# HGRN's first decays moved into ACT's, DVE's and POOL's queues ahead of its chunk loop, early tiles in DRAM, products queued at fixed places among the dense matmuls

## The chip, the cores and the metric

The kernel runs on one core of one Trainium2 chip. The metric is the device time of one execution in microseconds (us); before the change the median of three runs is 858.56 us (858.18 to 858.79). Engines: PE is TensorE (PEld its weight load), DVE VectorE, ACT ScalarE, POOL GpSimd, SP the queue that issues the weight loads. Each engine takes its instructions in the order that the build wrote, and stands when the first of them is not ready.

## The reference

One decoder layer over 512 tokens of width 1024, fp32. Two mixers run side by side on the same normed input, are merged by sigmoid gates, and a SwiGLU FFN follows. The change is in the mixers:

```
b = cumsum(log f)                       # HGRN2, 4 heads of 128, per chunk
decay[i,j] = exp(b_i - b_j), j <= i
attn = einsum(q_i, k_j, decay)
o = attn v + (q exp(b)) S
S = S exp(b_last) + (k exp(b_last - b))^T v
o_a = head_rms_norm(o) * silu(hg_g)

q, k = l2norm(silu(conv(q))), l2norm(silu(conv(k)))   # gated DeltaNet, 4 heads of 128
T = inverse(I + strict_lower(beta k k^T L))           # per chunk
v_new = u - w S;  o = qg S + (q k^T L) v_new;  S = S dl + kd^T v_new
o_b = head_rms_norm(o) * silu(dn_g)

merged = sigmoid(m_a) * (o_a Wa) + sigmoid(m_b) * (o_b Wb)
```

## The kernel before

Every dense product is made of three fp32r matmuls on a high and a low half of each operand (`mm3`). `dense_in` makes one feature tile (128 features by 512 tokens) at a time: `wload` loads 512 KB of weights (SP), casts the high half on ACT (whi, L108) and subtracts it on DVE (wlo, L109); 24 matmuls of 128x512 (two of L116 and one of L117 for each of eight rows of blocks) then fill one of three "mm" PSUM banks, and an evacuation (ACT, DVE or both) empties it. Three buffers each hold whi and wlo.

`mixers` writes the work down in program order, and a scheduler at build orders each engine's queue from it by its own estimate of when operands are ready; `high_priority` moves instructions forward, `issue_after` keeps one behind a named other one. So PE's queue is a fixed mixture: small products are set among dense matmuls. The stages around the change, with their place in the trace:

- 60 to 84 us: l2 norm of k (`l2`, `colsum`: square on ACT, split into halves by an ACT cast (L120) and a DVE subtraction, two matmuls with a matrix of ones (L376, L377) into a "dps" bank, Ln and Exp on ACT, multiplication on DVE) among the tiles of hg_f. `gates_late` (small exps of the DeltaNet gates, L337 to L347) reads gb, which comes by DMA. `dn_early` then builds k k^T and POOL's part begins: a copy through DRAM (L427, L429), 62 small substitution steps (`dn_sub`), and the copies of `dn_inv` through DRAM (L458 to L486), which end at 162 us.
- 84 to 177 us: dn_q, dn_v, dn_g, the l2 norm of q, `hg_prep` (HGRN's k and cumulative log decay b for four chunks on ACT and DVE, temporary "hct" tiles), hg_q's four tiles and two of hg_g (`qe`, `gge`), kept in six of the seven hct buffers; `dn_inv`'s products among the dense ones.
- 177 to 256 us: DeltaNet's `dn_prep` and four `dn_step`s in "dct" tiles (nine buffers), with the gate m_b0 among them, whose tiles go to DRAM (`gate_out`, early_b). POOL copies the early q and g out of the hct buffers into slots that come free (L792, L794): the slot of kT, which DeltaNet's last reads free, and that of qT.
- 256 to 370 us: HGRN. `hg_attn` makes one chunk's attention matrix: the diagonal and level 1 by two column sums, then for levels 64, 32, 16, 8, 4, 2 a tile E = exp(differences of b) (two subtractions on POOL, exp on ACT L660), multiplied on DVE by q in one half and by k in the other, and products of E with itself into one of two "hps" banks (L667 for 64 and 32, L673 for the rest), from which AT is patched (L669, L674). `hg_step` does output and state (L684, L693, L698, L704) and the head norm. The loop makes chunk c + 1's matrix beside chunk c's step. The dense work hg_g (two tiles), y_dn (`y_proj`) and m_b1 stands behind in program order, and the scheduler puts it where it believes PE free.

The rest (m_a, y_hg, merge, output projection, FFN, down projection) is not touched.

Of the kernel before, what the change touches and what calls it, by code (L numbers as in the profile page):

```python
# [43 lines left out]
class K:  # L44
# [324 lines left out]

    def colsum(self, sq, ct, ps, n=512, after=None):  # L370
# [4 lines left out]
        with self.tc.issue_after(after.ins) if after else nullcontext():  # L375
# [208 lines left out]
    def head_norm(self, c, o, gate, dst, ct, ps):  # L584
# [8 lines left out]
        sp = self.colsum(r, ct, ps)  # L593
# [36 lines left out]
    def hg_attn(self, c, out):  # L630
# [12 lines left out]
        E = self.hct((P, NH, 64))  # L643
# [8 lines left out]
        for lev in HG_LEVELS[:-1]:  # L652
            v = lambda x: x.rearrange("p h (n two t) -> p (h n) two t", two=2, t=lev)
            n = NH * P // (2 * lev)
            E = self.hct()
            Ev, bv, qv, kv = v(E), v(b), v(q), v(k)
            ref = bv[:, :, 0, lev - 1:lev].to_broadcast([P, n, lev])
            self.tt(Ev[:, :, 1, :], bv[:, :, 1, :], ref, ALU.subtract, nc.gpsimd)
            self.tt(Ev[:, :, 0, :], ref, bv[:, :, 0, :], ALU.subtract, nc.gpsimd)
            A.activation(E, E, AF.Exp)  # L660
            self.tt(Ev[:, :, 1, :], Ev[:, :, 1, :], qv[:, :, 1, :], ALU.mult)
            self.tt(Ev[:, :, 0, :], Ev[:, :, 0, :], kv[:, :, 0, :], ALU.mult)
            ps = self.hps()
# [8 lines left out]
            for h in range(NH):  # L672
                T.matmul(ps[:, h, :], E[:, h, :], E[:, h, :], start=True, stop=True)  # L673
# [3 lines left out]
    def hg_step(self, c, AT):  # L677
# [4 lines left out]
        o = self.hps()  # L682
        for h in range(NH):
# [41 lines left out]
    def mixers(self):  # L725
# [43 lines left out]
        for c in range(NC_):  # L769
            self.dn_prep(c)  # L770
# [530 lines left out]
```

## Time and profile before

| | |
|---|---|
| median of three runs | 858.56 us (858.18 to 858.79) |
| the profiled execution: time, span | 856.74 us, 855.0 us |
| mean granted clock of PE | 0.988 |
| busy: PE, DVE, ACT, POOL | 96%, 68%, 57%, 16% of the span |

The span runs from the first to the last instruction; the execution's own time is 1.7 us longer. A row of a timeline gives start, duration (the sum over xN instructions of a row that holds several), engine, line, operation, out<-in, shape, and in brackets how long the engine stood before and what released it. PE's busy time is modelled from starts, so two neighbours overlap in the rows; the distance of starts is what one costs. A clock of 1.00 is the higher of TensorE's two levels (2.4 GHz), 0.5 the lower (1.2).

### The profile page before, as it was taken

The numbers are of one execution on the slowest core, as the hardware profiler recorded it, in microseconds if no ns is written. First come the engines' busy times: TensorE is split into PE (matmuls) and PEld (weight loads), VectorE is DVE, ScalarE is ACT, GpSimd is POOL, SyncE is SP. The second block draws the span as 40 slices with busy tenths as digits, with TensorE's granted clock in tenths as the row PEclk, the third lists the DMA queues.
The fourth block names the chain that finished last, engine by engine and source line by source line (L and its number), as shares of the span: only waits on it lengthen the run. The fifth ranks groups of instructions, "written<-read, shape, count | busy, mean of one in ns | idle before, by whom it ended". The sixth has DMA issues, their size and how long they took to land.

```text
span 855.0 us, 12316 instructions
## 1 busy us (share of the span) xinstructions
PE 821.0 (96%) x4677; PEld 689.3 (81%) x4677; DVE 585.6 (68%) x903; ACT 485.4 (57%) x884; POOL 136.9 (16%) x187
## 2 busy tenths in 40 slices
PE   9998999999997999899999999999999998999995
PEld 8886887767876877788888898999999997876774
DVE  4794998625557788862664797787787787557545
ACT  6658798945376466585443365545455456445443
POOL 1420178300034245430010300000000000000000
PEclk9998999999999999999999999999999999999999
DMA  8425532712126112253211313322413404556552
GB/s 294 153 94 177 140 108 74 179 51 74 38 86 209 51 49 87 87 173 97 86 53 49 123 50 100 116 82 99 145 54 99 148 24 141 181 172 206 186 175 99
DMA packets 34907, 98.53 MB, mean 115 GB/s; under 512 B 4192, under 2 KB 4608, under 8 KB 34720
## 3 DMA queue, kind: packets, MB, share of 16 engines
q1 hardware_dynamic: 32112, 88.65, 31.5%
q0 software_dynamic: 2736, 9.09, 4.0%
q8 instruction: 37, 0.61, 0.3%
q14 instruction: 22, 0.18, 0.1%
HBM read 91.95 MB, written 5.78 MB: 114 GB/s over the span
## 4 chain that ended last, share of the span: by engine, by line
PE 66%; DVE 12%; DMA 11%; ACT 6%; issue 3%; POOL 0%; SPq 0%; DVEq 0%; ACTq 0%; POOLq 0%
PE mm L116 20%; PE mm L117 11%; DMA raw<-in_w_down_dram 8%; DVE wlo L109 3%; PE hps L116 3%; ACT whi L108 3%; DVE hct L146 3%; PE hps L1041 2%; PE hps L1040 2%; PE hps L1042 2%; PE hps L117 2%; DVE s L149 2%; PE hps L673 2%; DVE s L146 1%; PE mm L898 1%
## 5 line engine op out<-in xcount | busy, mean ns | idle before, releaser
L116 PE MATMUL mm<-s,whi 128*128 128x512 f32 (+1 forms) x992 | 310.5, 392 | 0.0
L109 DVE TENSOR_TENSOR wlo<-raw,whi 128x1024 fp32r<-128x1024 f32 x108 | 135.5, 1254 | 116.2 <-ACT whi L108 111.7
L116 PEld LDWEIGHTS mm<-s,whi 128*128 128x128 f32 x992 | 184.3, 190 | 36.5 <-issue 0.2
L117 PE MATMUL mm<-s,wlo 128*128 128x512 f32 (+1 forms) x496 | 196.9, 397 | 0.2 <-DVE wlo L109 0.2
L108 ACT CAST whi<-raw 128x1024 fp32r<-128x1024 f32 x108 | 113.1, 1047 | 80.2 <-DMA raw<-in_w_down_dram 37.9
L117 PEld LDWEIGHTS mm<-s,wlo 128*128 128x128 f32 x496 | 94.0, 189 | 20.2 <-DVE wlo L109 0.7
L146 POOL TENSOR_TENSOR s<-s,dct 128x512 f32<-128x512 f32 (+1 forms) x9 | 12.7, 1437 | 391.0 <-DVE s L149 362.1
L120 ACT CAST whi<-raw 128x512 fp32r<-128x512 f32 (+1 forms) x64 | 38.9, 617 | 28.2 <-PE mm L1041 10.1
L120 ACT CAST whi<-s 128x512 fp32r<-128x512 f32 x42 | 25.9, 617 | 49.4 <-PE mm L116 23.6
L1040 PE MATMUL hps<-s,whi 128*128 128x256 f32 x168 | 47.2, 281 | 0.4 <-DVE hct L146 0.4
L1041 PE MATMUL hps<-s,whi 128*128 128x256 f32 x168 | 47.2, 281 | 0.1
L1042 PE MATMUL hps<-s,wlo 128*128 128x256 f32 x168 | 46.9, 279 | 0.0
L146 DVE TENSOR_TENSOR wlo<-raw,whi 128x512 fp32r<-128x512 f32 (+1 forms) x64 | 43.5, 688 | 2.4 <-ACT whi L120 1.6
L146 POOL TENSOR_TENSOR hct<-s 128x256 f32<-128x256 f32 (+1 forms) x55 | 38.2, 724 | 25.8 <-DVE hct L146 8.6
L116 PE MATMUL hps<-s,whi 128*128 128x512 f32 (+1 forms) x144 | 40.8, 368 | 0.0
L146 DVE TENSOR_TENSOR hct<-hct,s 128x256 f32<-128x256 f32 (+1 forms) x63 | 35.0, 601 | 4.6 <-ACT hct L624 2.0
L146 POOL TENSOR_TENSOR s<-s 128x126 f32<-128x126 f32 (+22 forms) x62 | 34.8, 561 | 10.5 <-DMA s<-scr 5.7
L1040 PEld LDWEIGHTS hps<-s,whi 128*128 128x128 f32 x168 | 31.5, 188 | 0.9 <-DVE hct L146 0.6
L1041 PEld LDWEIGHTS hps<-s,whi 128*128 128x128 f32 x168 | 31.7, 188 | 0.6 <-DVE s L146 0.3
L1042 PEld LDWEIGHTS hps<-s,wlo 128*128 128x128 f32 x168 | 31.7, 189 | 0.0
L1041 PE MATMUL mm<-s,whi 128*128 128x256 f32 x112 | 31.5, 281 | 0.0
L1040 PE MATMUL mm<-s,whi 128*128 128x256 f32 x112 | 31.4, 281 | 0.0
(325 smaller groups left out, 1850.0 us busy)
## 6 DMA issues: line engine op xcount, KB each, us to landing
raw<-in_w_in_a_dram SPq DMA_DIRECT2D x44, 512.0 KB, 3.4
raw<-in_w_down_dram SPq DMA_DIRECT2D x44, 512.0 KB, 3.4
s<-in_w_gu_dram SPq DMA_DIRECT2D x56, 256.0 KB, 4.1
raw<-in_w_gu_dram SPq DMA_DIRECT2D x16, 512.0 KB, 3.6
raw<-in_w_o_dram SPq DMA_DIRECT2D x8, 512.0 KB, 3.5
dct<-in_w_out_dram SPq DMA_DIRECT2D x16, 256.0 KB, 4.2
raw<-in_w_iab_dram SPq DMA_DIRECT2D x8, 260.0 KB, 5.9
s<-in_xT_dram SPq DMA_DIRECT2D x8, 256.0 KB, 6.0
```

Source lines behind the costliest of these rows:

```text
L108: nc.scalar.copy(hi[:, :n], raw[:, :n])
L109: nc.vector.tensor_tensor(out=lo[:, :n], in0=raw[:, :n], in1=hi[:, :n].bitcast(F32), op=ALU.subtract)
L116: return [mm(ps, lh, rh, start=start, stop=False), mm(ps, lh, rl, start=False, stop=False), mm(ps, ll, rh, start=False, stop=stop)]
L117: mm(ps, ll, rh, start=False, stop=stop)]
L120: self.nc.scalar.copy(hi, src)
L146: (eng or self.nc.vector).tensor_tensor(out=out, in0=a, in1=b, op=op)
L149: self.nc.vector.scalar_tensor_tensor(out=out, in0=a, scalar=s, in1=b, op0=op0, op1=op1)
L673: T.matmul(ps[:, h, :], E[:, h, :], E[:, h, :], start=True, stop=True)
L898: T.matmul(ps, mh, wl, start=False, stop=False)
L1040: mm(ps, wh[:, k, :], ah[k], start=start and k == 0, stop=False, skip_group_check=True)
L1041: mm(ps, wh[:, k, :], al[k], start=False, stop=False, skip_group_check=True)
L1042: mm(ps, wl[:, k, :], ah[k], start=False, stop=k == 3, skip_group_check=True)
```

## The change

1. `l2` of q is written after dn_g, its column sums tied to dn_g's matmuls 6, 18, 30, 42 instead of dn_v's 38, 50, 62, 74. `gates_late` is kept behind the last instructions of the l2 norm of k.
2. Early tiles of hg_q, hg_g and m_b0 go through one "out" buffer (`spill`) to DRAM (POOL's queue, early_q, early_g); five DMAs bring q and g back (L817, L818) where the six POOL copies stood.
3. The hct buffers are thus free, and `hg_decay` makes E times k for levels 64, 32, 16, 8, 4 of chunk 0 right behind `dn_inv` in program order; `hg_attn` then multiplies by q alone.
4. The tiles of HGRN's steps come from dct and dps.
5. hg_g's last tiles, y_dn and m_b1 are written ahead of the HGRN loop, and every group of HGRN's products is `paced`: at high priority behind the next of the marks, every fourth of those dense matmuls from the ninth on.

```diff
+FIRST, PACE = 8, 4
...
+    def spill(self):
+        return self.tp.tile([P, 512], F32, tag="out", name=self.name("out"), bufs=1)
...
+    @contextmanager
+    def paced(self):
+        with self.tc.high_priority(), self.tc.issue_after(next(self.marks).ins):
+            yield
...
-        with self.tc.issue_after(after.ins) if after else nullcontext():
+        with self.paced() if after == "mark" else self.tc.issue_after(after.ins) if after else nullcontext():
...
+            m = nc.vector.tensor_tensor(out=y[:, h, :], in0=y[:, h, :], in1=t, op=ALU.mult)
+        return e, m
...
+    def hg_decay(self, c, lev):
+        v = lambda x: x.rearrange("p h (n two t) -> p (h n) two t", two=2, t=lev)
+        n = NH * P // (2 * lev)
+        E = self.hct()
+        Ev, bv, kv = v(E), v(self.hf[:, c]), v(self.hk[:, c])
+        ref = bv[:, :, 0, lev - 1:lev].to_broadcast([P, n, lev])
+        self.tt(Ev[:, :, 1, :], bv[:, :, 1, :], ref, ALU.subtract, self.nc.gpsimd)
+        self.tt(Ev[:, :, 0, :], ref, bv[:, :, 0, :], ALU.subtract, self.nc.gpsimd)
+        self.nc.scalar.activation(E, E, AF.Exp)
+        self.tt(Ev[:, :, 0, :], Ev[:, :, 0, :], kv[:, :, 0, :], ALU.mult)
+        return E
+    def hg_attn(self, c, out, decays={}):
...
-        pr = self.hct()
+        pr = self.dct()
         self.tt(pr, k, q, ALU.mult, nc.gpsimd)
-        ps = self.colsum(pr.rearrange("p h t -> p (h t)"), self.hct, self.hps)
+        ps = self.colsum(pr.rearrange("p h t -> p (h t)"), self.dct, self.hps, after="mark")
...
-            A.activation(E, E, AF.Exp)
+            E = decays[lev] if lev in decays else self.hg_decay(c, lev)
+            Ev, qv = v(E), v(q)
...
-            self.tt(Ev[:, :, 0, :], Ev[:, :, 0, :], kv[:, :, 0, :], ALU.mult)
...
+            with self.paced():
+                for h in range(NH):
...
-        o = self.hps()
-        for h in range(NH):
-            T.matmul(o[:, h, :], vv(h), AT[:, h, :], start=(h == 0), stop=(c == 0), skip_group_check=True)
+        o = self.dps()
+        with self.paced():
...
+        norm = self.l2(self.kT, False, [self.log["hg_f"][i] for i in (30, 34, 38, 42)])
         self.dn_early()
         self.dense_in("hg_f", cm(self.hf), fts=range(2, 4))
-        self.gates_late()
+        with self.tc.issue_after(norm[0].ins), self.tc.issue_after(norm[1].ins):
+            self.gates_late()
...
-        self.l2(self.qT, True, [self.log["dn_v"][i] for i in (38, 50, 62, 74)])
         self.gdn = self.slot(5, [P, NH, S])
         self.dense_in("dn_g", self.gate_evac(self.gdn, self.dnw))
-        early, eg = {}, {}
+        self.l2(self.qT, True, [self.log["dn_g"][i] for i in (6, 18, 30, 42)])
+        early_q, early_g, early_b = (self.dp.tile([n, P, S], F32, name=f"early_{t}") for n, t in ((4, "q"), (2, "g"), (4, "b")))
         def qe(i, ps):
-            early[i] = self.hct((P, 512))
-            A.copy(early[i], ps)
+            t = self.spill()
+            A.copy(t, ps)
+            nc.gpsimd.dma_start(out=early_q[i], in_=t)
         def gge(i, ps):
-            eg[i] = self.hct((P, 512))
-            self.sigmoid(eg[i], ps)
-            self.stt(eg[i], ps, self.hnw, eg[i], ALU.mult, ALU.mult)
+            t = self.spill()
+            self.sigmoid(t, ps)
+            self.stt(t, ps, self.hnw, t, ALU.mult, ALU.mult)
+            nc.gpsimd.dma_start(out=early_g[i], in_=t)
...
+        early_e = {lev: self.hg_decay(0, lev) for lev in HG_LEVELS[:5]}
...
-            t = self.hct((P, 512))
+            t = self.spill()
...
-        for i in range(4):
-            nc.gpsimd.tensor_copy(self.hq[:, :, i, :], early[i].rearrange("p (c t) -> p c t", c=NC_))
-        for i in range(2):
-            nc.gpsimd.tensor_copy(self.ghg[:, i, :], eg[i])
+        for c in range(NC_):
+            nc.gpsimd.dma_start(out=self.hq[:, c], in_=early_q[:, :, c * P:c * P + P].rearrange("f p t -> p f t"))
+        nc.gpsimd.dma_start(out=self.ghg[:, :2], in_=early_g.rearrange("f p t -> p f t"))
+        self.dense_in("hg_g", self.gate_evac(self.ghg, self.hnw), fts=range(2, 4))
...
+        self.y_proj(0, self.odn, y_dn)
...
+        self.dense_in("m_b1", gate_b)
+        dense = self.log["hg_g"][48:] + self.log["y0"] + self.log["m_b1"]
+        self.marks = iter(dense[FIRST::PACE])
         at = []
-        run(self.hg_attn(0, at))
-        self.dense_in("hg_g", self.gate_evac(self.ghg, self.hnw), fts=range(2, 4))
+        run(self.hg_attn(0, at, early_e))
...
-                    self.mm3(ps, wh[:, k, sl], wl[:, k, sl], o[0][:, k, :], o[1][:, k, :], k == 0, k == 3)
-                evac(ch * 2 + f2, ps)
+                    self.log.setdefault(f"y{m}", []).extend(
+                        self.mm3(ps, wh[:, k, sl], wl[:, k, sl], o[0][:, k, :], o[1][:, k, :], k == 0, k == 3))
+                with self.tc.high_priority():
+                    evac(ch * 2 + f2, ps)
```

Where the instructions stand in the queues follows from the build. First POOL's queue behind `dn_inv`'s last substitution steps, before (rows of L458 to L486, then early_b and the copies) and now. s6_92 is hf, HGRN's b; scr1 and scr2 are in DRAM; hct_286 to hct_290 are the decays of the five levels.

Before:

```order
L458 COPY s15_119_787<-s15_119_787 128x512
L460 DMA scr1_649<-s15_119_787 64x32x16 x2
L462 DMA scr2_650<-s15_119_787 64x16x32 x2
L483 DMA s14_253_1793<-scr1_649 32x16x32 x2
L486 DMA s10_118_786<-scr2_650 128x8x128 x2
L786 DMA early_b_2239<-hct_350_2271 128x512
L786 DMA early_b_2239<-hct_355_2307 128x512
L792 COPY s11_366_2384<-hct_227_1620 128x4x128
```

Now:

```order
L493 DMA s14_253_1802<-scr1_649 32x16x32 x2
L496 DMA s10_118_786<-scr2_650 128x8x128 x2
L151 TENSOR_TENSOR hct_286_1979<-s6_92_672 128x4x64 x2
L151 TENSOR_TENSOR hct_287_1984<-s6_92_672 128x8x32 x2
L151 TENSOR_TENSOR hct_288_1989<-s6_92_672 128x16x16 x2
L151 TENSOR_TENSOR hct_289_1994<-s6_92_672 128x32x8 x2
L151 TENSOR_TENSOR hct_290_1999<-s6_92_672 128x64x4 x2
L782 DMA early_q_1464<-out_227_1623 128x512
L782 DMA early_q_1464<-out_232_1657 128x512
```

The ten subtractions stand behind the last two scratch DMAs and ahead of the DMAs of early_q.

Next ACT at the weights of the second hg_q tile (whi_229), before and now. mm_201 and mm_189 are tiles of dn_g, s5 the gate, hct_216 to hct_218 tiles of hg_prep's chunks.

Before:

```order
L143 ACTIVATE s5_193_1323<-s5_193_1323 128x512
L611 ACTIVATE hct_217_1543<-hct_217_1543 128x512
L141 ACTIVATE dct_219_1569<-s7_160_1134 128x512
L612 ACTIVATE hct_217_1543<-hct_217_1543,one_75 128x512
L108 CAST whi_229_1623<-raw_228_1622 128x1024
L141 ACTIVATE s5_193_1323<-mm_205_1400 128x512
```

Now:

```order
L630 ACTIVATE hct_218_1552<-s6_92_672,sm_86_639 128x128
L649 ACTIVATE hct_286_1979<-hct_286_1979 128x512
L113 CAST whi_229_1627<-raw_228_1626 128x1024
L146 ACTIVATE s5_177_1275<-mm_189_1352 128x512
L633 ACTIVATE hct_218_1552<-hct_218_1552 128x512
L147 ACTIVATE s5_177_1275<-s5_177_1275,one_75 128x512
L634 ACTIVATE hct_218_1552<-hct_218_1552,one_75 128x512
L148 ACTIVATE s5_177_1275<-s5_177_1275 128x512
L649 ACTIVATE hct_287_1984<-hct_287_1984 128x512
L649 ACTIVATE hct_288_1989<-hct_288_1989 128x512
L649 ACTIVATE hct_289_1994<-hct_289_1994 128x512
L649 ACTIVATE hct_290_1999<-hct_290_1999 128x512
```

The exp of hct_286 stands ahead of whi_229; four more stand ahead of the reading of the last dn_g tile's bank. Further on come the next weight casts, the Ln of three of q's column sums and, as the 25th instruction from the first exp on, the cast of dct_207 for the fourth.

DVE, which the same stretch waits for, has now:

```order
L631 TENSOR_SCALAR s6_92_672<-s6_92_672,sm_85_638,sm_84_637 128x128 x4
L151 TENSOR_TENSOR hct_286_1979<-hct_286_1979,s13_210_1467 128x4x64
L114 TENSOR_TENSOR wlo_230_1628<-raw_228_1626,whi_229_1627 128x1024
L151 TENSOR_TENSOR hct_218_1552<-hct_218_1552,s6_92_672 128x512
L154 SCALAR_TENSOR_TENSOR s5_177_1275<-mm_189_1352,dnw_86,s5_177_1275 128x512
L637 SCALAR_TENSOR_TENSOR s6_92_672<-onesr_73,hct_218_1552 128x128 x4
```

The multiplication of hct_286 by k stands ahead of wlo_230 (second hg_q tile) and of the evacuation of mm_189.

Last PE, at the second hg_q tile (mm_231) and the column sum of q's fourth head, now:

```order
L122 MATMUL mm_231_1632<-s0_63_567,wlo_230_1628 128x512
L121 MATMUL mm_231_1632<-s0_63_567,whi_229_1627 128x512
L387 MATMUL dps_209_1458<-dct_207_1454,onesr_73 128x512
L121 MATMUL mm_231_1632<-s2_65_569,whi_229_1627 128x512
L122 MATMUL mm_231_1632<-s0_63_567,wlo_230_1628 128x512
L121 MATMUL mm_231_1632<-s1_64_568,whi_229_1627 128x512
L121 MATMUL mm_231_1632<-s3_66_570,whi_229_1627 128x512
```

Ten dense matmuls of mm_231 stand ahead of the column sum dps_209; before, this pair stood among the matmuls of the first dn_g tile.

## Rows read from the trace of the kernel before

**Rows 1.** The page, busy time, share and instructions of each engine.

```profile
PE 821.0 (96%) x4677; PEld 689.3 (81%) x4677; DVE 585.6 (68%) x903; ACT 485.4 (57%) x884; POOL 136.9 (16%) x187
```

**Rows 2.** Stretches: length, each engine's busy time (instructions), PE's clock, DMA share, GB/s.

```profile
60.00:80.00 20.00, 16.72 (x61) 12.85 (x60) 12.52 (x20) 16.39 (x29) 1.99 (x3) 0.83 0.61 210
180.00:200.00 20.00, 20.00 (x151) 12.98 (x149) 6.24 (x8) 7.94 (x22) 0.00 (x0) 1.00 0.15 53
400.00:420.00 20.00, 20.00 (x88) 16.18 (x87) 7.89 (x9) 11.00 (x15) 0.00 (x0) 1.00 0.25 82
262.00:370.00 108.00, 97.53 (x578) 78.20 (x577) 87.97 (x139) 62.23 (x112) 48.81 (x67) 0.97 0.26 86
```

**Rows 3.** DVE's timeline, 70 us: start, duration, instruction [idle before, releaser].

```profile
69.65 0.18 DVE L341 COPY sm<-s 128x16 f32<-128x16 f32 x1 [4.71 <-DMA s<-gd]
```

**Rows 4.** PE's timeline, 74 to 84 us, same columns.

```profile
74.23 0.80 PE L377 MATMUL dps<-dct,onesr 128*128 128x512 f32 x1 [1.26 <-DVE dct L146]
...
75.25 1.06 PE L116 MATMUL mm<-s,whi 128*128 128x512 f32 x2
...
83.27 0.63 PE L116 MATMUL mm<-s,whi 128*128 128x512 f32 x2
```

**Rows 5.** ACT's timeline, 71 us.

```profile
71.33 0.62 ACT L120 CAST dct<-dct 128x512 fp32r<-128x512 f32 x1
```

**Rows 6.** POOL's timeline, 157 to 275 us.

```profile
157.30 0.66 POOL L483 DMA_DIRECT2D s<-scr  x1 [3.19 <-DMA scr<-s]
...
160.19 1.80 POOL L486 DMA_DIRECT2D s<-scr  x2 [1.38 <-DMA scr<-s]
...
245.91 2.29 POOL L792 COPY s<-hct 128x512 f32<-128x512 f32 x4 [5.28 <-PE dps L556]
...
268.32 7.48 POOL L146 TENSOR_TENSOR hct<-s 128x256 f32<-128x256 f32 x12
```

**Rows 7.** PE's timeline, 131 to 164 us.

```profile
131.98 0.40 PE L376 MATMUL dps<-dct,onesr 128*128 128x512 f32 x1
...
141.36 0.50 PE L377 MATMUL dps<-dct,onesr 128*128 128x512 f32 x1 [1.51 <-DVE dct L146]
141.69 0.40 PE L117 MATMUL mm<-s,wlo 128*128 128x512 f32 x1
...
163.24 0.40 PE L117 MATMUL mm<-s,wlo 128*128 128x512 f32 x1
```

**Rows 8.** ACT's timeline, 133 to 149 us.

```profile
133.48 1.25 ACT L387 ACTIVATE dct<-dps,eps 128x512 f32<-128x512 f32 x2
...
146.73 1.05 ACT L108 CAST whi<-raw 128x1024 fp32r<-128x1024 f32 x1 [0.42 <-PE mm L116]
147.68 0.59 ACT L141 ACTIVATE s<-mm 128x512 f32<-128x512 f32 x1
148.17 0.62 ACT L623 ACTIVATE hct<-hct 128x512 f32<-128x512 f32 x1
148.69 0.71 ACT L142 ACTIVATE s<-s,one 128x512 f32<-128x512 f32 x1
```

**Rows 9.** PE's timeline, 256 to 345 us.

```profile
256.15 0.50 PE L377 MATMUL dps<-dct,onesr 128*128 128x512 f32 x1 [1.05 <-DVE dct L146]
...
275.47 1.69 PE L667 MATMUL hps<-hct 128*64 128x64 f32 x16 [4.71 <-DVE hct L146]
...
281.23 0.55 PE L667 MATMUL hps<-hct 128*32 128x32 f32 x8
...
344.10 0.65 PE L667 MATMUL hps<-hct 128*64 128x64 f32 x8 [1.98 <-DVE hct L146]
```

**Rows 10.** The tile early_b, from the issue of its DMAs to their landing.

```profile
DMA to landing us min/median/max: 3.5/4.4/7.2
```

**Rows 11.** DVE's timeline, 270 us.

```profile
270.22 6.87 DVE L146 TENSOR_TENSOR hct<-hct,s 128x256 f32<-128x256 f32 x6 [1.17 <-ACT hct L660]
```

**Rows 12.** One chunk of HGRN, the instructions of line 116 alone.

```profile
309.74:333.46 23.72, 11.68 (x34) 6.15 (x33) 1.00 0.18 57
```

More of the change, by code (lines that the diff above doesn't have):

```diff
@@ L1 @@
 import math
-from contextlib import ExitStack, nullcontext
+from contextlib import ExitStack, contextmanager, nullcontext
 import numpy as np
@@ L582, in dn_step, with head_norm @@
         return self.head_norm(c, o, self.gdn, self.odn, self.dct, self.dps)
-    def head_norm(self, c, o, gate, dst, ct, ps):
+    def head_norm(self, c, o, gate, dst, ct, ps, after=None):
         nc = self.nc
@@ L681, in hg_step @@
         vv = lambda h: self.vhg[:, c, h * P:h * P + P]
-        o = self.hps()
-        for h in range(NH):
-            T.matmul(o[:, h, :], vv(h), AT[:, h, :], start=(h == 0), stop=(c == 0), skip_group_check=True)
+        o = self.dps()
+        with self.paced():
+            for h in range(NH):
+                T.matmul(o[:, h, :], vv(h), AT[:, h, :], start=(h == 0), stop=(c == 0), skip_group_check=True)
         if c < NC_ - 1:
-            kd = self.hct()
+            kd = self.dct()
             self.tt(kd, b[:, :, P - 1:P].to_broadcast([P, NH, P]), b, ALU.subtract, nc.gpsimd)
@@ L690, in hg_step @@
             self.tt(kd, kd, k, ALU.mult)
-            ps = self.hps()
-            for h in range(NH):
-                T.transpose(ps[:, h, :], kd[:, h, :], self.ident)
-            kt = self.hct()
+            ps = self.dps()
+            with self.paced():
+                for h in range(NH):
+                    T.transpose(ps[:, h, :], kd[:, h, :], self.ident)
+            kt = self.dct()
             A.copy(kt, ps)
-            ps = self.hps()
-            for h in range(NH):
-                T.matmul(ps[:, h, :], kt[:, h, :], vv(h), start=True, stop=True)
+            ps = self.dps()
+            with self.paced():
+                for h in range(NH):
+                    T.matmul(ps[:, h, :], kt[:, h, :], vv(h), start=True, stop=True)
         A.activation(b, b, AF.Exp)
@@ L702, in hg_step @@
             self.tt(q, q, b, ALU.mult)
-            for h in range(NH):
-                T.matmul(o[:, h, :], self.Sh[:, h, :], q[:, h, :], start=False, stop=True, skip_group_check=True)
+            with self.paced():
+                for h in range(NH):
+                    T.matmul(o[:, h, :], self.Sh[:, h, :], q[:, h, :], start=False, stop=True, skip_group_check=True)
         if c < NC_ - 1:
@@ L825, in mixers @@
         self.dense_in("m_b1", gate_b)
+        dense = self.log["hg_g"][48:] + self.log["y0"] + self.log["m_b1"]
+        self.marks = iter(dense[FIRST::PACE])
+        at = []
+        run(self.hg_attn(0, at, early_e))
+        self.ohg = [self.slot(7 + i, [P, NH, S], F32R) for i in range(2)]
+        for c in range(NC_):
+            nxt = self.hg_attn(c + 1, at) if c + 1 < NC_ else iter(())
+            for _ in range(3):
+                next(nxt, None)
+            n = self.hg_step(c, at[c])
+            next(n)
+            run(nxt)
+            run(n)
         self.ma = [self.slot((6, 13)[i], [P, NH, S]) for i in range(2)]
```

40 lines of the change are left out of this document (9 added, 31 removed).

## The prediction, made before the changed kernel was run

> **What bounds the kernel now.** I read the page's busy shares first: TensorE (PE) is busy 821.0 of 855.0 us [rows 1]. So a change can only win where PE stands still or runs at its lower clock, and can only lose by making it stand elsewhere. Next the table by stretches [rows 2]. From 180 to 200 us PE is busy all 20.00 us; from 400 to 420 it finishes 88 dense matmuls in 20 us, 0.227 us each; ahead of the HGRN stretch 93 of them take 21.55 us, 0.232 each [rows 7]. I use 0.2305. Between 60 and 80 us PE is busy 16.72 us and its granted clock is 0.83. In the HGRN stretch, 262 to 370 us, it is busy 97.53 of 108 us while DVE is busy 87.97. Those two stretches and the one between them (130 to 177 us) are where the edits act, so I read each engine's timeline there. Differences from no change of up to 0.2%, 1.7 us, are what a measurement of this kernel can't tell.
>
> **The l2 norm of k (edit: the late gates follow the norm).** DVE stands 4.71 us for a DMA into gd before gates_late's copy (L341), with the norm's work queued behind it [rows 3]. PE then waits 1.26 us for the second column sum at 74.23, and its dense matmuls run at half speed, 1.06 us for two instead of 0.63; the stretch ends at 83.27 [rows 4]. Without the copy ahead of them the first cast (71.33 plus 0.62, less about 0.1 for a gate instruction that stood ahead of it) still comes last, so PE resumes at about 71.8 [rows 5]. With nothing in its way it issues the same 24 dense matmuls and 6 column sums in 30 x 0.2305 = 6.9 us and ends at 78.7. I take **-4.6 us**. If the first wait alone is enough to lower the clock, the half-speed part (74.23 to about 79.5, so 2.6 us lost) stays and -2.0 remains; more than -4.7, the whole stand of DVE, is not to be had. Everything up to the next stretch moves by this, POOL's dn_inv chain too, which hangs on the normalised k.
>
> **The hold by the early decays.** "Made during the DeltaNet steps" is not what the order shows. The ten subtractions stand in POOL's queue behind all of dn_inv's scratch copies; but ACT's first exp (hct_286) stands ahead of the weights of the second hg_q tile, and DVE's first multiply ahead of the same tile's wlo and of the evacuation of the third dn_g tile (mm_189). Both engines take their rows in order, so both stand until POOL delivers. When is that? POOL ends its last scratch copy at 160.19 + 1.80 = 162.0 [rows 6]; less 4.6 this is 157.4. Two subtractions at 7.48 / 12 = 0.62 each [rows 6] make it 158.65. The weight cast nine rows ahead of the exp, before at 146.73 [rows 8], comes at about 142, so ACT reaches the exp near 144 and stands some 14 us.
>
> PE goes on with what is prepared: three banks and the weights cast before. dn_g begins at 131.98 - 4.6 = 127.4 [rows 7]; five tiles (four of dn_g, one of hg_q, 120 matmuls) and six column sums put the end at 156.5. The second hg_q tile then wants a bank and weights that come after the exp: some 7 us of waiting. Ten matmuls into that tile stands the fourth head's column sum of l2(q), whose cast is the 25th ACT instruction from the exp on: 3 weight casts at 0.95, 3 reads of PSUM at 0.49, 3 Ln from PSUM at 0.62 and 16 others at 0.52 [rows 8] make 14.5 us. So this column sum comes at 158.65 + 14.5 = 173.2 instead of 156.5 + 2.3 = 158.8, and with its pair PE stands at 173.7.
>
> Before, the same point comes at 141.69 + 94 x 0.2305 + 2.3 = 165.7 [rows 7]. This comparison contains the -4.6 above and the 1.51 us wait for the fourth column sum (141.36), which goes because it moved. The position is thus **+8.0 us**. After 4.71 us of standing at 275.47 PE ran at its lower level until about 281.4, 5.9 us, of which half (2.95) was lost [rows 9]; I add **+2.95** for the same behind two stands of 7 us. Early total: **+11.0**. Lower bound +8 (the clock stays up), upper +15.6 (POOL's chain does not move by the 4.6). What hides a hold is only the prefetch of three banks, and that is counted.
>
> **HGRN's q and g through DRAM.** POOL's six copies (the four of q begin at 245.91, after 5.28 us of waiting for PE's last read of kT [rows 6]) go; in their place POOL issues four DMAs and one more at the same release. 256 KB on this queue took 3.5 to 7.2 us to land, median 4.4 [rows 10], so q is there at about 250.5. DVE's five decay multiplies by q now stand ahead of the splits of the last two DeltaNet norms, for one of which PE already waits 1.05 us at 256.15 [rows 9]; at 1.1 us each (6.87 / 6, [rows 11]) they take 5.5 us, to 256.0. With the split itself behind them, that makes the column sum about 1.5 us later than 256.15: **+1.5**, between -1 (landing in 3.5) and +3. The Trainium skill (DMA: Bandwidth & Descriptors, "Anatomy of one DMA — SWDGE (gpsimd) path") fits 2.0 us plus bytes over 436e3 for a DMA of this path: an estimate of 2.6 us here, by which the 1.5 would vanish and the time be 859.2. The shortest landing of the trace, 3.5 us, is above it, so the measurement decides. Against the change speaks the trap in the Trainium skill (SBUF — State Buffer, "SBUF: two separate sides"), that busy DVE modes can starve such a DMA of descriptors; with the longest landing of the rows the term would be +4.3 and the time 863.5; no row here shows the trap apart from other causes.
>
> The spills themselves (six DMAs on a POOL that was idle until 223 us, each tile 5.5 us of PE work apart, one buffer) I cost at nothing: landing takes 4.4, less than a tile. Without that cover each would hold an ACT copy by its excess.
>
> **The HGRN stretch.** From 262 to 370 us PE stands 108 - 97.53 = 10.5 us [rows 2], of which 4.71 at 275.47 and 1.98 at 344.10 [rows 9]; with the 2.95 of the lower clock 13.4 us is all there is to win, since PE's instructions stay the same in number. Three things change. The ten subtractions and five exps of chunk 0, behind which DVE's six multiplies took 6.87 us [rows 11] and PE stood 4.71, are made already. Dense work is spread between the groups, four matmuls each. And the steps' tiles come from another ring, so POOL and ACT may run ahead. Does DVE keep up? A chunk now takes 23.72 us with 34 dense matmuls of the high half of the weights [rows 12] and half as many of the low half, 51, 11.8 us, which leaves 12 for products and waits; afterwards a chunk holds some 14 groups and 56 dense, 12.9 us, so 21 to 25 us of PE work. DVE is busy 87.97 / 108 = 81% of the stretch [rows 2], 19.3 us of such a chunk, so PE is last by a little. I allow 1.5 us of remaining waits and 1.5 us of further switches between the two kinds of matmul: 13.4 - 3.0, **-10.4**. Bounds: -13.4, and -3 if DVE stays behind in every chunk.
>
> **Sum:** +11.0 + 1.5 - 10.4 = +2.1 us. The profiled execution took 856.74 us (its span 855.0), so 858.8 in that measure; the median of the runs shown is 858.56, so the forecast is **860.7 us**.
>
> **The rivals.**
> - *The hold is covered* (other side: faster). The decisive point: POOL delivers the first decay before PE has used up its banks, or ACT has slack enough to catch up within a tile, so that PE waits under 2 us. Then -4.6 - 1.5 remain of the early part, and with -10.4 and +1.5 the time is 843.6, range 842 to 850. For it: 120 matmuls of prefetched work. Against it: POOL's last copy ends at 162.0 [rows 6], 25 ACT instructions wait behind. Chance 0.13.
> - *The hold costs less than counted* (clock stays up, or part of the 25 instructions is overlapped) and HGRN gives all: +11.0 falls to +6 or +8, 853 to 857. Chance 0.17.
> - *The queue of the products becomes the wait.* A group queued at a fixed place in PE's order stops all dense work behind it if DVE is late; before, the scheduler put the groups where it believed them ready. DVE is at 81% of the stretch [rows 2], so if it loses as much again to waits for ACT and PE, each chunk ends where it did, and the stretch gives only 3: 860.7 + 7.4 = 868, range 866 to 872. Chance 0.15.
> - *The decays do not lie in the DeltaNet steps at all*: this is the forecast's own case, since by the order they lie in dn_inv's dense tiles.
>
> **How the numbers follow.** The forecast has 0.55, its own range 855.5 to 866.5 (early part +8 to +14, HGRN -7 to -12, [rows 2, 9]). To hold 8 in 10 the range reaches from 850 to 868. Faster than 856.8: all of the first rival, three quarters of the second and 0.08 of the forecast, 0.34. Within 0.2%: 0.11 of the forecast and the rest of the second, 0.15. Slower: the remaining 0.36 of the forecast and the third, 0.51.
>
> **What would show it.** Right: ACT idle for over 10 us before an exp of L649 near 145 to 158, released by POOL; PE idle in two pieces ahead of and inside the second hg_q tile; a granted clock near 0.85 from 160 to 180 instead of 1.00; no wait of DVE at L341 and a clock near 1 from 60 to 80; PE's 4.71 us stand before chunk 0's products gone; under 4 us of PE waits in the HGRN stretch. Wrong: PE close to 20 of 20 us between 140 and 180, which makes the first rival; or PE waiting for DVE before the queued groups in each chunk, which makes the third.

## The result and the profile after

The changed kernel takes 862.53 us (median of 14 runs, 857.75 to 867.85), the kernel before beside it 858.19 us (14 runs, 852.20 to 859.17). The ratio is 1.006 (95% interval 1.0041 to 1.0079): 0.6% slower. The forecast was 860.7 us, in a range of 850 to 868, with a chance of 0.51 for slower.

The profiled execution of the change took 857.75 us (span 856.0), the fastest of its 14; the one of before took 856.74 (855.0). So the two traces differ by 1.0 us where the medians differ by 4.3, and one more profile of the changed kernel (c1 below, 861.77 us) is needed to read the usual case.

First the page's busy shares of the change: PE is no more busy than before [rows 1], POOL is by 9 us.

```profile
PE 818.6 (96%) x4677; PEld 690.3 (81%) x4677; DVE 586.4 (69%) x903; ACT 484.2 (57%) x884; POOL 146.2 (17%) x192
```

Then its stretches, with the columns of rows 2 (length, busy time of PE, PEld, DVE, ACT and POOL with their instructions, PE's clock, DMA share, GB/s):

```profile
60.00:80.00 20.00, 18.17 (x79) 14.29 (x78) 13.33 (x19) 19.28 (x33) 1.99 (x3) 1.00 0.58 210
160.00:180.00 20.00, 12.30 (x45) 8.82 (x46) 13.68 (x21) 16.77 (x29) 3.80 (x6) 0.58 0.27 92
300.00:320.00 20.00, 17.97 (x110) 14.69 (x110) 18.31 (x25) 9.44 (x18) 13.20 (x14) 1.00 0.17 53
320.00:340.00 20.00, 17.64 (x105) 14.87 (x104) 18.50 (x32) 11.19 (x20) 10.76 (x12) 1.00 0.17 54
340.00:360.00 20.00, 20.00 (x126) 16.90 (x125) 13.70 (x25) 9.71 (x17) 3.72 (x7) 0.91 0.43 143
```

Three of the same stretches before the change:

```profile
160.00:180.00 20.00, 20.00 (x146) 14.22 (x144) 7.86 (x13) 13.82 (x27) 1.80 (x2) 1.00 0.44 132
300.00:320.00 20.00, 18.17 (x107) 14.03 (x105) 17.33 (x30) 12.63 (x22) 9.87 (x13) 1.00 0.13 46
320.00:340.00 20.00, 19.53 (x123) 15.71 (x119) 18.04 (x31) 13.02 (x24) 9.04 (x12) 1.00 0.25 80
```

From 60 to 80 us the clock is up where it was at 0.83 [rows 2]. From 160 to 180, where PE was busy all 20.00 us before, it is busy 12.30 at a clock of 0.58: that is the hold. From 300 to 340 DVE is busy 18.3 and 18.5 of 20 us (before 17.3 and 18.0), PE 18.0 and 17.6 (before 18.2 and 19.5).

ACT's timeline of the change at the hold (start, duration, instruction, idle before and its releaser):

```profile
145.24 0.39 ACT L630 ACTIVATE hct<-s,sm 128x128 f32<-128x128 f32 x1
157.15 0.63 ACT L649 ACTIVATE hct<-hct 128x512 f32<-128x512 f32 x1 [11.53 <-POOL hct L151]
157.69 1.03 ACT L113 CAST whi<-raw 128x1024 fp32r<-128x1024 f32 x1
...
171.65 0.64 ACT L125 CAST dct<-dct 128x512 fp32r<-128x512 f32 x1
```

POOL's timeline at the same place:

```profile
153.45 0.66 POOL L493 DMA_DIRECT2D s<-scr  x1 [0.20 <-DMA scr<-s]
154.10 1.80 POOL L496 DMA_DIRECT2D s<-scr  x2
155.92 7.13 POOL L151 TENSOR_TENSOR hct<-s 128x256 f32<-128x256 f32 x10
```

DVE's:

```profile
157.81 3.10 DVE L151 TENSOR_TENSOR hct<-hct,s 128x256 f32<-128x256 f32 x1 [11.50 <-ACT hct L649]
...
163.52 0.74 DVE L154 SCALAR_TENSOR_TENSOR s<-mm,dnw,s 128x512 f32<-128x512 f32 x1
```

ACT stands 11.53 us before the first early exp, released by POOL, whose subtractions begin when its last scratch copy has been issued, at 155.9 (before: 162.0, [rows 6]). DVE stands 11.50 behind ACT, and the evacuation of the third dn_g tile (163.52) behind that. DVE's first multiplication took 3.10 us, where the same form takes 0.41 at 273.41, while POOL's subtractions ran on to 163.05; e2 comes back to this. PE's timeline of the change shows what this costs:

```profile
150.05 0.40 PE L387 MATMUL dps<-dct,onesr 128*128 128x512 f32 x1
...
156.73 0.40 PE L122 MATMUL mm<-s,wlo 128*128 128x512 f32 x1
164.31 1.22 PE L121 MATMUL mm<-s,whi 128*128 128x512 f32 x2 [7.19 <-DVE s L154]
...
168.32 0.63 PE L121 MATMUL mm<-s,whi 128*128 128x512 f32 x1
172.33 0.80 PE L387 MATMUL dps<-dct,onesr 128*128 128x512 f32 x1 [3.39 <-ACT dct L125]
...
178.75 0.62 PE L121 MATMUL mm<-s,whi 128*128 128x512 f32 x2
```

Two stands, 7.19 us for that evacuation and 3.39 for the cast at 171.65, and dense matmuls at half speed from 164.31 to about 177.3. The second hg_q tile ends at 178.7. From 156.96, where PE had used up what was prepared, its 24 matmuls, the pair of column sums and one small product would have taken 6.4 us, to 163.3: **the hold costs 15.4 us**.

At HGRN, PE's timeline of the change has these stands left, where before had 4.71, 1.98 and smaller ones [rows 9]:

```profile
263.87 0.50 PE L388 MATMUL dps<-dct,onesr 128*128 128x512 f32 x1 [2.30 <-DVE dct L151]
...
274.65 0.39 PE L387 MATMUL hps<-dct,onesr 128*128 128x256 f32 x1 [1.03 <-ACT dct L125]
...
313.42 0.65 PE L685 MATMUL hps<-hct 128*64 128x64 f32 x8 [1.12 <-DVE hct L151]
314.98 0.41 PE L685 MATMUL hps<-hct 128*32 128x32 f32 x8 [0.91 <-DVE hct L151]
...
339.83 0.65 PE L685 MATMUL hps<-hct 128*64 128x64 f32 x8 [2.36 <-DVE hct L151]
```

The output projection begins at 437.21 us in the change and 434.31 before. Up to the end of the second hg_q tile the change is 9.3 us behind (178.7 against 169.4, which is 118 dense matmuls at 0.2317 and a product after 141.69, [rows 7]); so 6.4 us come back behind that. The profiled execution is lucky in one place, the k norm; this is PE's timeline there in the profile of the change taken again:

```profile
73.47 0.50 PE L387 MATMUL dps<-dct,onesr 128*128 128x512 f32 x1 [3.65 <-ACT dct L125]
...
74.90 1.05 PE L121 MATMUL mm<-s,whi 128*128 128x512 f32 x2
```

Its ACT's timeline:

```profile
68.92 1.05 ACT L113 CAST whi<-raw 128x1024 fp32r<-128x1024 f32 x1 [1.62 <-DMA raw<-in_w_in_a_dram]
```

The weights' DMA lands later, ACT casts at 68.92 and not at 67.38, PE stands 3.65 us and not 1.83, and its clock falls behind that; the column sums of q begin at 153.13 instead of 150.05.

### The profile page after: what moved, and what is told of

It is laid out like the page before. It is cut to its first block, busy times and chain, and to the rows that moved or that the text cites. A ratio compares the mean times of both kernels' runs of the same rounds, so it can differ in the third digit from the quotient of the medians.

```text
span 856.0 us, 12307 instructions
## 1 busy us (share of the span) xinstructions
PE 818.6 (96%) x4677; PEld 690.3 (81%) x4677; DVE 586.4 (69%) x903; ACT 484.2 (57%) x884; POOL 146.2 (17%) x192
## 4 chain that ended last, share of the span: by engine, by line
PE 57%; DMA 11%; DVE 7%; ACT 5%; POOL 5%; issue 3%; DVEq 0%; ACTq 0%; POOLq 0%
PE mm L121 15%; DMA raw<-in_w_down_dram 8%; PE mm L122 8%; POOL s L151 4%; PE hps L121 3%; ACT whi L113 3%; DVE wlo L114 3%; PE hps L1069 2%; PE hps L1068 2%; PE hps L1070 2%; PE mm L927 2%; PE mm L925 2%; PE mm L926 2%; PE hps L122 2%; PE hps L692 2%
## 5 line engine op out<-in xcount | busy, mean ns | idle before, releaser
L125 ACT CAST whi<-raw 128x512 fp32r<-128x512 f32 (+1 forms) x64 | 38.9, 617 | 29.2 <-PE mm L1069 10.1
L151 POOL TENSOR_TENSOR hct<-s 128x256 f32<-128x256 f32 x48 | 39.1, 847 | 5.4 <-PE hps L685 4.6
L151 DVE TENSOR_TENSOR hct<-hct,s 128x256 f32<-128x256 f32 (+1 forms) x52 | 29.7, 624 | 14.0 <-ACT hct L649 11.5
```

The lines of the kernel that those rows point to most:

```text
L125: self.nc.scalar.copy(hi, src)
L151: (eng or self.nc.vector).tensor_tensor(out=out, in0=a, in1=b, op=op)
```

## The experiments

Twelve kernels ran, in four sets, each beside the kernel before. Two starts on PE serve as marks: M1, the first of q's three column sums (150.05 in the change), behind which the hold lies, and M2, the start of the output projection (437.21). M1 varies from one execution to the next with the k norm; M2 - M1 hardly does (287.2 and 287.6 in two profiles of the change).

| kernel | M1 | M2 | M2 - M1 | ratio to before (95%) | median us (before) |
|---|---|---|---|---|---|
| the change, first profile | 150.05 | 437.21 | 287.2 | 1.006 (1.0041 to 1.0079) | 862.53 (858.19) |
| c1, the change again | 153.13 | 440.69 | 287.6 | 1.0084 (1.0058 to 1.0111) | 863.91 (856.45) |
| e1, no early decays | 150.98 | 432.65 | 281.7 | 0.9998 (0.9981 to 1.0015) | 856.68 (856.89) |
| e2, decays late | 151.44 | 431.52 | 280.1 | 0.9956 (0.9938 to 0.9973) | 853.60 (856.89) |
| e3, late gates free | 154.78 | 442.11 | 287.3 | 1.0072 (1.0044 to 1.01) | 863.96 (856.89) |
| e4, not paced | 152.91 | 442.52 | 289.6 | 1.0086 (1.0068 to 1.0103) | 864.39 (856.89) |
| e5, e2 and subtractions late | 150.03 | 427.11 | 277.1 | 0.9905 (0.9879 to 0.9931) | 848.64 (856.45) |
| e6, e5 and q behind the norms | 152.61 | 428.23 | 275.6 | 0.9932 (0.9907 to 0.9957) | 850.95 (856.45) |
| e7, e6 and late gates free | 153.99 | 428.03 | 274.0 | 0.9951 (0.9929 to 0.9973) | 851.83 (856.45) |
| e8, multiplications late | 153.01 | 442.09 | 289.1 | 1.0094 (1.006 to 1.0128) | 863.91 (855.43) |
| e9, subtractions in a gap | 152.72 | 436.75 | 284.0 | 0.9994 (0.9975 to 1.0013) | 854.78 (855.43) |
| e10, e6 and a later start | 154.10 | 420.47 | 266.4 | 0.9839 (0.9809 to 0.9869) | 841.89 (855.43) |
| e11, the change and a later start | 153.09 | 434.59 | 281.5 | 1.0006 (0.9982 to 1.003) | 855.18 (855.03) |

**c1, the change again.**

> The changed kernel itself once more, beside the kernels of this set: 1.006 times the kernel before, 861 to 863 if that takes 857. Its profile shows which of its stands vary from one execution to the next: the hold (7.2 and 3.4 us) in every one by theory, the half clock behind the l2 norm of k only in some.

863.91 us, 0.9 above the range named; the ratio's interval overlaps that of the first measurement. Gains against the change are counted below from its 1.006, the smaller of the two. The stands of the hold are 7.42 and 3.39 us, as in the first profile; what varied is the k norm (above).

**e1, no early decays.**

```diff
-        early_e = {lev: self.hg_decay(0, lev) for lev in HG_LEVELS[:5]}
+        early_e = {}
```

> The early decays of chunk 0 are not made; hg_attn makes them in its loop. Theory (the hold is the loss): ACT no longer stands 11.5 us before 157 us and PE's 7.2 and 3.4 us stands and the half clock behind them go, about -8.5; in the HGRN stretch chunk 0's products wait again for ten POOL subtractions, +3 to +7. Sum 862.5 - 8.5 + 5 = 859, range 856 to 861. Rival (the loss lies in the HGRN stretch or in the DRAM round trip): the early part gives nothing back, 863 to 870.

Measured 856.68 us, within the theory's range: M2 - M1 falls by 5.5 us (5.9 against c1). The hold is gone, and chunk 0 pays for it in the HGRN stretch. This is its DVE's timeline there:

```profile
256.93 7.86 DVE L151 TENSOR_TENSOR dct<-dct,s 128x256 f32<-128x256 f32 x1
...
265.47 0.41 DVE L151 TENSOR_TENSOR dct<-dct,s 128x256 f32<-128x256 f32 x1
```

POOL's:

```profile
257.10 5.38 POOL L151 TENSOR_TENSOR hct<-s 128x256 f32<-128x256 f32 x9
```

And PE's:

```profile
266.37 0.58 PE L387 MATMUL hps<-dct,onesr 128*128 128x256 f32 x1 [7.00 <-ACT dct L125]
```

A multiplication of 256 columns takes 7.86 us, where the same form takes 0.41 a moment later, and PE stands 7.00 us behind it. POOL has nine subtractions in that time, then issues a DMA and multiplies until 264.50.

**e2, the decays late.** In `gge` the last sigmoid activation is kept as `self.ga`, its product on DVE as `self.gv`:

```diff
-        early_e = {lev: self.hg_decay(0, lev) for lev in HG_LEVELS[:5]}
+        with self.tc.issue_after(self.ga.ins), self.tc.issue_after(self.gv.ins):
+            early_e = {lev: self.hg_decay(0, lev) for lev in HG_LEVELS[:5]}
```

> The decays are made early, but their exps and DVE multiplications are kept behind the evacuation of the second early hg_g tile, some 60 us later; POOL's subtractions stay. Theory: the whole hold goes and chunk 0's early decays stay, 862.5 - 8.5 = 854, range 852 to 856, and PE is busy nearly all of 140 to 180 us with the clock at 1.00. Rival (the DMA and PSUM chain of dn_inv is next in line at the same place): PE stands there for other reasons and the time stays within 2 us of 862.5.

853.60 us, as the theory has it. But PE does not work through: it stands 4.21 us for DVE at 164.11, and the clock is at 0.91 from 160 to 180. DVE's timeline of this kernel:

```profile
157.06 1.72 DVE L401 TENSOR_TENSOR s<-s,dct 128x512 f32<-128x512 f32 x2 [0.93 <-ACT dct L399]
158.84 5.21 DVE L151 TENSOR_TENSOR dct<-dct,dct 128x512 fp32r<-128x512 f32 x1
163.98 1.74 DVE L114 TENSOR_TENSOR wlo<-raw,whi 128x1024 fp32r<-128x1024 f32 x1
```

POOL's:

```profile
158.79 7.39 POOL L151 TENSOR_TENSOR hct<-s 128x256 f32<-128x256 f32 x10
```

PE's:

```profile
164.11 0.56 PE L388 MATMUL dps<-dct,onesr 128*128 128x512 f32 x1 [4.21 <-DVE dct L151]
```

The split of the fourth head's square took 5.21 us, from 158.84 on, while POOL's ten subtractions ran from 158.79 to 166.2.

**e5, POOL's subtractions late too.** The third DMA of early_q is kept as `self.gp`:

```diff
-        with self.tc.issue_after(self.ga.ins), self.tc.issue_after(self.gv.ins):
+        with self.tc.issue_after(self.gp.ins), self.tc.issue_after(self.ga.ins), self.tc.issue_after(self.gv.ins):
```

> As with the decays late, and POOL's ten subtractions moved too, from behind the scratch copies to behind the third DMA of early_q (some 20 us later). In the profile of the decays late one DVE subtraction of 512 columns (q's fourth head) took 5.21 us at 158.84 instead of 0.69, exactly while POOL's ten subtractions ran, and PE stood 4.21 us for it. Theory (POOL and DVE keep each other out): that stand and the clock behind it go, 853.6 - 4.2 - 1 = 848.5, range 847 to 850. Rival (the DVE instruction waited for its operand and the 5.2 us are a fault of the record): 853 to 854.

848.64 us: the theory's. The same split, in DVE's timeline, now takes what it takes elsewhere:

```profile
157.43 0.69 DVE L151 TENSOR_TENSOR dct<-dct,dct 128x512 fp32r<-128x512 f32 x1 [0.47 <-ACT dct L125]
```

The collision has only moved. POOL's ten subtractions and a DVE subtraction that makes a wlo (1.23 us at 165.29) now meet later:

```profile
174.53 5.97 POOL L151 TENSOR_TENSOR hct<-s 128x256 f32<-128x256 f32 x10
```

```profile
175.00 6.58 DVE L114 TENSOR_TENSOR wlo<-raw,whi 128x1024 fp32r<-128x1024 f32 x1 [1.97 <-PE dps L489]
```

But there PE does not wait for it, and works through the stretch; two of its stretches, columns as above:

```profile
160.00:180.00 20.00, 20.00 (x184) 13.57 (x182) 9.69 (x8) 13.65 (x31) 6.56 (x12) 1.00 0.32 110
240.00:260.00 20.00, 17.32 (x75) 13.79 (x75) 11.26 (x18) 13.77 (x24) 7.78 (x11) 0.83 0.40 119
```

The whole of the hold is gone here (15.4 us), but M2 - M1 is only 10.1 lower: in this profile the clock falls to 0.83 from 240 to 260 behind PE's stand for q, 2.69 us, and to 0.91 twice in HGRN, where the first profile of the change had lost it once. Part of what is won early is given back so.

**e8, only the multiplications late.** The multiplication by k in `hg_decay` for chunk 0's early levels is kept behind `self.gv`; exps and subtractions stay.

> Only DVE's five multiplications by k are kept until behind the second early hg_g tile; ACT's exps and POOL's subtractions stand as in the change. Theory (the hold that counts is ACT's row: 25 ACT instructions behind the first exp set the column sum of q's fourth head): PE's first stand shrinks by some 2 us, the second grows by as much, the time is that of the change, 861 to 864. Rival (DVE's row, with the evacuation behind it, sets the end): 854 to 858.

863.91 us, the change's time. PE's first stand is 6.81 us, the second 4.41 (c1: 7.42 and 3.39). They move by 0.6 and 1.0 us, less than the 2 expected, and nothing is won: the end of the hold is set by ACT's row, not DVE's.

**e9, the subtractions in a gap.** The decays are written ahead of `dn_inv`, and both loops of DMAs that read the scratch back are kept behind the last subtraction; one of them:

```diff
+            with self.tc.issue_after(self.dl.ins):
+                nc.gpsimd.dma_start(out=T0[L, :, :, L].rearrange("p c h t -> p (c h) t"), in_=self.full[1][L, :, L])
```

> POOL's ten subtractions stand ahead of the DMAs that read dn_inv's scratch back, in the 2.8 us in which POOL waits for the scratch to land, instead of behind them; the order of ACT, DVE and PE is word for word that of the change. Theory (the hold ends when POOL delivers): the first exp comes 6 us earlier (ACT stands 5.5 us, not 11.5), the time falls by 5 to 8 us with the clock, 854.5 to 857.5. Rival (dn_inv's scratch, now read back some 4.3 us later, is next in line): 860 to 863.

854.78 us, as by the theory. ACT's timeline:

```profile
153.17 0.63 ACT L651 ACTIVATE hct<-hct 128x512 f32<-128x512 f32 x1 [4.99 <-POOL hct L650]
```

PE's:

```profile
169.12 0.80 PE L387 MATMUL dps<-dct,onesr 128*128 128x512 f32 x1 [7.01 <-ACT dct L125]
```

ACT stands 4.99 us instead of 11.53; of PE's two stands the first is gone, and the second hg_q tile ends 22.6 us behind M1 instead of 28.7. With the other engines' queues in the same order, the time follows POOL's delivery. In this profile M2 - M1 is only 3.2 us lower; its clock is at 0.91 in three stretches of HGRN (the change: one).

**e3 and e7, the late gates.** In both `self.gates_late()` stands without its two `issue_after`.

> gates_late is again free to stand ahead of the l2 norm of k. Theory: DVE stands some 4.7 us for the DMA again, PE loses 4.6 us before 84 us and POOL's chain, on which the hold hangs, comes 4.6 later too: 862.5 + 4.6 = 867, range 865.5 to 868. Rival (the hold's end is set by something other than POOL's chain, so the 4.6 us only move PE's stand from one place to another): 862.5 to 863.5.

> As the one before, with gates_late free to stand ahead of the l2 norm of k, as in the kernel before. Theory (the term of the k norm is 4.6 us, of which 2.6 are the clock): 4 to 5 us more than the one before. Rival (PE's clock falls behind the 1.9 us stand that remains in both, so only the second stand counts): 1.5 to 2.5 us more.

Both miss. The medians move by less than their intervals: e3's ratio 1.0072 lies between the change's 1.006 and 1.0084, e7's is 0.0019 above e6's. The stand for gd, 4.71 us before the change [rows 3], does not come back; DVE's timelines of e3 and of e7:

```profile
66.89 0.17 DVE L346 COPY sm<-s 128x16 f32<-128x16 f32 x1 [1.42 <-DMA s<-gd]
```

```profile
66.06 0.18 DVE L346 COPY sm<-s 128x16 f32<-128x16 f32 x1 [0.96 <-DMA s<-gd]
```

In both gd is there some 3 us earlier than in the profile of before, and ACT's weight cast comes late instead (69.36 and 68.73, behind stands of 1.45 and 1.20 us for the DMA). Over the eleven profiles with the gates behind the norm M1 lies between 150.03 and 154.10, 152.2 in the mean; over the two without, 154.4. So an estimate of what the edit is worth is 2.2 us. In six of the eleven the cast waits for its DMA too, and M1 comes 84.1 to 84.2 us behind the cast; in e3 and e7 it comes 85.4 and 85.3 behind: where the weights are late, the edit is worth 1.2 us. Only the change's first profile and e5 keep the whole gain; in the other nine, work ahead of the norm is late, mostly the weights' DMA.

**e4, not paced.** `paced` yields without priority or `issue_after`.

> HGRN's products are no longer queued at marks; the scheduler places them by its own estimate, with all else as changed. Theory (PE waits less because the groups are spread): the HGRN stretch loses 3 to 7 us, 865.5 to 869.5. Rival (the gain of that stretch comes from the early decays and the rings alone, pacing gives nothing): 861.5 to 863.5. If a queued group holds dense work back: 856 to 861.

864.39 us, between the ranges of theory and rival; M2 - M1 is 2.0 to 2.4 us above the two profiles of the change. Queueing the groups is worth about that by the profiles, less than the theory's 3 to 7; by the ratios (1.0086 against 1.006 and 1.0084) it is not shown.

**e6, q behind the norms.** The multiplications by q of the early levels are kept behind the last DeltaNet norm's split on DVE.

> As with the subtractions late, and DVE's five multiplications by q are kept behind the split of the last DeltaNet norm. Theory (the DRAM round trip of q is what that norm's column sum waits for, 2.30 us at 256.81 in the profile of the decays late): that stand goes, 2 to 4 us with the clock behind it, 848.5 - 3 = 845.5. Rival (the multiplications are then late for chunk 0's own products, and PE stands there instead): 848 to 850.

850.95 us, not told apart from e5 (the intervals overlap); it lies 1 us above the rival's range and 5 above the theory's. PE's stand at that norm is 1.10 us, about that of before (1.05, [rows 9]), instead of 2.30 to 2.69, and the next stand, for chunk 0's own column sum, is 2.13 instead of 0.90. So 1.2 us move by one place.

**e10 and e11, a later start.** In both:

```diff
-FIRST, PACE = 8, 4
+FIRST, PACE = 24, 4
```

> As with q behind the norms, and HGRN's groups begin at the 25th dense matmul instead of the ninth, so each stands 16 dense matmuls (3.7 us) later. Theory (DVE is late for groups queued at fixed places; in that profile PE stands 2.1, 1.1, 0.9 and 2.4 us for them): these stands shrink by 3 to 4 us in all, 851 - 3 = 848, range 846.5 to 849. Rival (DVE takes longer than PE per chunk, so the lateness returns by the last chunk, or the products then outlast the dense work): 850 to 852.

> The change with one number altered: HGRN's groups begin at the 25th dense matmul instead of the ninth. Theory (the start is worth the same whether the hold is there or not, some 8 to 9 us, since the stands for DVE in the HGRN stretch and the half clock behind them are the same in both): 862.3 - 8.5 = 854, range 852 to 856, with the stands of 7.2 and 3.4 us at the hold unchanged. Rival (what the later start gained came from q's multiplications behind the norms as well): 857 to 861.

e10, on e6, took 841.89 us, 1.6% under the kernel before and the best of all; M2 - M1 falls by 9.2 us, three times what was expected. e11, on the change, took 855.18 us, inside the expected range; but by the ratios that is 4.6 us less than the change (6.7 less than c1; M2 - M1: 5.7 to 6.1), not the "8 to 9" of its theory. Three stretches of e6, columns as above:

```profile
260.00:280.00 20.00, 17.87 (x101) 13.96 (x99) 16.27 (x22) 9.29 (x18) 10.99 (x14) 0.91 0.32 114
300.00:320.00 20.00, 17.97 (x109) 14.45 (x109) 18.36 (x30) 10.63 (x21) 10.06 (x11) 0.91 0.16 54
320.00:340.00 20.00, 17.63 (x100) 14.04 (x99) 16.46 (x25) 12.47 (x23) 13.30 (x16) 0.91 0.21 68
```

The same three of e10:

```profile
260.00:280.00 20.00, 19.90 (x123) 15.74 (x123) 18.74 (x27) 11.79 (x24) 13.15 (x17) 1.00 0.41 145
300.00:320.00 20.00, 17.85 (x124) 14.81 (x123) 17.81 (x30) 10.32 (x20) 9.92 (x11) 1.00 0.16 54
320.00:340.00 20.00, 18.91 (x115) 15.32 (x114) 16.11 (x29) 14.34 (x26) 11.79 (x15) 1.00 0.29 91
```

In e6 the clock is at 0.91 in these three stretches, in e10 at 1.00: the stands there (1.05, 1.10 and 1.09 us instead of 2.13, 1.12, 0.91 and 2.36) cost no clock. An estimate: a mean of 0.91 over 20 us is 3.6 us at half speed, 1.8 us lost, 5.4 in three stretches; with the 3.3 us by which the stands shrank that makes 8.7 of the 9.2. The change had lost it in one stretch only (0.91 from 340 to 360), so e11 had less to win. DVE is no less busy; it only has more time before the first group is due.

## Why the prediction was right, and where it was off

**The sign and its cause stand.** The text asked for ACT standing over 10 us for POOL, from about 145 to 158, for two stands of PE ahead of and inside the second hg_q tile, and for a clock near 0.85 from 160 to 180; the profile has 11.53 us, 7.19 and 3.39 us, and 0.58: the lower clock takes in both stands, not only what follows the second. That the hold is the loss, and not the HGRN stretch, is shown: e2 and e5 take it away and gain 9 and 13 us against the change (by the ratios), e9 takes 6.1 us off it with one queue's order altered and gains 6, e8 leaves ACT's row and gains nothing. The decays lie where the order had them, ahead of the DeltaNet steps. The rival that the hold is covered falls, and so does the one by which HGRN gives only 3. (The second rival's price is off: by its own terms +6 and +8 give 855.7 and 857.7, not 853 to 857.) What the moved l2 norm of q, and the steps' tiles in dct and dps, are worth alone, no run shows.

**The hold: +17.4 forecast (173.2 - 158.8 = 14.4, and 2.95 for the clock), +15.4 measured.** POOL was free at 155.9, not at 157.4 (in this profile, which has the whole gain of the k norm): it no longer waited for its last scratch copy (1.38 us, [rows 6]). The 25 ACT instructions took 172.3 - 157.15 = 15.1 us against 14.5, and behind the second stand the clock, at half until about 177.3, cost 2.4 against 2.95.

**The k norm: -4.6 forecast, -2.2 on average (an estimate from the profiles).** The failing step is "nothing in its way". The term was read from one execution, in which gd came late (the copy at 69.65, [rows 3]) and the weights in time (the cast at 67.3). In the change's first profile it is there in full: PE resumes at 71.92 at the higher clock. Where the weights land 1 to 1.6 us later, PE stands longer and runs at half speed even with the gates out of the way; and in e3 and e7, with the gates in the way, gd was there early. The lower bound given, -2.0, is about the usual case. This is also most of why the profile pair differs by 1.0 us and the medians by 4.3.

**DRAM: +1.5 forecast, +1.25 measured** (2.30 us of standing against 1.05, [rows 9]). q was landed 4.5 us after POOL's issue at 253.84, when DVE's first multiplication began at 258.37. The four reads of q took 4.7 us in the median from issue to landing; the spills of q, as large and on the same queue, 2.3. The fit in the Trainium skill (DMA: Bandwidth & Descriptors, "Anatomy of one DMA — SWDGE (gpsimd) path"), an estimate of 2.6 us for each, is near the spills and not near the reads; what makes the difference no run shows. The longest landing of rows 10, from which the text took 863.5, is not one of 256 KB; the DMAs of early_b before the change, with size and median time:

```profile
early_b<-hct POOLq DMA_DIRECT2D x4, 256.0 KB, 4.1
s<-early_b POOLq DMA_DIRECT2D x1, 1024.0 KB, 7.2
```

The multiplications themselves took 1.9 us, not 5.5. The 1.1 us for each was read from six that ran beside POOL's twelve subtractions (268.32 to 275.80, [rows 6, 11]); these five ran with no such work on POOL. The two errors of the step, a shorter run and the wait for the DMA itself, largely cancelled.

**HGRN: -10.4 forecast, about -7.7 measured** (6.4 us come back behind the hold, after 1.25 lost to q). The step that failed is the 1.5 us allowed for remaining stands: they were 1.03, 1.12, 0.91 and 2.36, 5.4 in all, and over the 4 us named as the sign. DVE, which I put at 81% and PE "last by a little", is busy 18.3 and 18.5 of 20 us from 300 to 340: with the groups at fixed places it is last there, and e10 and e11 win by giving it a later start. The third rival's mechanism is thus real, at a third of its price.

Summed, +2.1 + 2.4 (k norm) - 2.0 (hold) - 0.25 + 2.7 (HGRN) = +5.0, against 4.3 in the medians and 0.6%, 5.1 us, by the ratio. The sign came from the mechanism; that 862.53 lies so near 860.7 is in part luck, for two terms were too low and two too high, and the loss itself is about twice the +2.1 forecast.

## What to carry to other kernels

An early start for work that hangs on a slow engine is no gain if its consumers are queued ahead of urgent work: look, in each in-order queue, at what stands behind the moved instruction, and when its operand really comes. The same edit one place later (e2, e5) turned 0.6% of loss into 0.4 and 1.0% of gain. A queue paced at fixed marks wants a head start for its slowest feeder: sixteen matmuls more ahead of the first group brought 0.9% (e10 against e6), more than all else in that kernel (0.7%), and 0.5% on the change as it stood (e11). And an edit priced from one execution should be checked against the spread of the place it stands in.

## What the runs showed of the hardware

A DVE instruction that reads two tiles of SBUF (the on-chip memory that the engines share) can wait through several POOL instructions, not one: a subtraction of 128x512 took 5.21 us (e2), one of 128x1024 6.58 (e5) and a multiplication of 128x256 7.86 (e1) while POOL's subtractions ran one behind the other, against 0.69, 1.23 and 0.41 without them. e5 shows it by moving POOL's work alone: the split is back at 0.69, and the instruction that now meets the subtractions is long instead. POOL pays too: its ten took 5.97 us in e5, where DVE got in only at their end, and 7.39 in e2 and 7.13 in the change, where DVE got in between. The Trainium skill (SBUF — State Buffer, "Who interferes with whom") says that a DVE instruction with two SBUF inputs contends with a GpSimd instruction that reads SBUF, and that whoever comes first has the shared ports for the whole instruction; that DVE waits through a run of seven or more of POOL's is more than it says, and is what these rows show. In the change DVE got in sooner (3.10 us at 157.81), so a wait through the whole run is not the rule.

PE's clock does not fall behind every stand of one length: after 2.30 us at the last norm the next column sum took 0.50 us in the change (263.87) and 0.79 in e2 (256.81):

```profile
256.81 0.79 PE L388 MATMUL dps<-dct,onesr 128*128 128x512 f32 x1 [2.30 <-DVE dct L151]
```

And the stands of 1.12 and 0.91 us from 300 to 320 left it at 1.00 in the change and at 0.91 in e6. What decides between them was not settled. From e6 to e10 9.2 us were won where the stands shrank by 3.3; by the estimate under e10 the clock was worth more than the stands.
